# Eight experts worked in an order ranked on the chip, four of them with both halves of their tokens side by side

## The chip, the cores and the metric

The kernel runs on one core of one Trainium2 chip. Its engines are TensorE (PE, with its weight loads as PEld), VectorE (DVE), ScalarE (ACT), GpSimd (POOL) and SyncE (SP), which here only issues transfers. The metric is the time of one execution in device microseconds (us), the median of several runs. The profile is of one execution, whose own time and span are given beside it.

## What is computed

Two layers over 256 latent and 256 context tokens of width 1024. Nearly all of the change lies in the last part of the second layer, a mixture of eight experts of which each token takes two:

```python
def moe_swiglu(h, router, w_gate_up, w_down):
    logits = (h @ router).astype(jnp.float32)
    top_logit, top_idx = lax.top_k(logits, TOP_K)
    top_w = jax.nn.softmax(top_logit, axis=-1)
    gates = jnp.sum(jax.nn.one_hot(top_idx, N_EXPERTS, dtype=jnp.float32) * top_w[..., None], axis=-2).astype(h.dtype)
    out = jnp.zeros_like(h)
    for e in range(N_EXPERTS):
        out = out + gates[..., e:e + 1] * swiglu(h, w_gate_up[e], w_down[e])
    return out
```

`h` is 256 x 1024, an expert's `w_gate_up` 1024 x 7168 and its `w_down` 3584 x 1024, all float32. An expert's weights are 42 tiles of 1 MiB.

## The kernel before

A float32 product is made of three passes: each operand is split into a rounded high half (`fp32r`) and the low rest, and `mm3` (L121) adds hi x hi, hi x lo and lo x hi in PSUM. Weights come through `weights` (L111): a 1 MiB transfer from SyncE into a `raw` tile, a ScalarE copy into `whi` (L108), a VectorE subtraction into `wlo` (L109). In the expert stage there are six raw tiles (one of them in the unused half of `x`) and three pairs of `whi` and `wlo`. SyncE issues in program order and waits for VectorE to have read a raw tile before it fills it again.

In `experts` the router's logits give each token's two experts (`sel`), a count of earlier tokens (`slot`) gives its place in the expert, and `onehot` (L1089) makes from it a 0/1 matrix. `gather` (L1096) multiplies it with the normalized tokens, so that up to 128 of an expert's tokens stand in the columns of `xe` (a high and a low part); `hotT` is its transpose. `run` (L1190) goes through experts 0 to 7 in that order, seven chunks of 512 inner columns each. A chunk is `up` (L1127: gate and up products, 4 x 4 blocks, 48 matmuls of 512 columns), Silu times up into one of two scratch tiles (`spare`, L1083), `turned` (L1147: four transposes and a split into `eahi`, `ealo`) and, one chunk later, `down` (L1156: 24 matmuls into the two banks `y`). In an expert's fifth chunk the next one is gathered; after its last, `finished` and `scatter` add its result, weighted by `gate`, to the tokens in `acc`.

`weigh` (L1052) makes the gate weights and the largest count `mosti`; its small VectorE operations are put among the splits after the first chunk. At the end SyncE and the others read `mosti`, and if an expert has over 128 tokens, the whole round runs a second time (`over` = 1). The order of the instructions on each engine is fixed at build time by a scheduler that follows the program's order and the readiness that it assumes; `issue_after` holds a piece back until a named instruction.

Of the kernel before, what the change touches and what calls it, by code (L numbers as in the profile page):

```python
# [36 lines left out]
EC = DE // 512  # L37
BIG = 3.0e38
# [11 lines left out]
class Trunk:  # L50
# [887 lines left out]
    def experts(self):  # L938
        nc, tc, ins = self.nc, self.tc, self.ins
        with ExitStack() as es:  # L940
# [52 lines left out]
            early = [self.weights(ins["moegu"][0, 0, 0, kh], 2048, pieces=range(4), by=by) for kh, by in ((0, None), (1, nc.gpsimd))]  # L993
# [53 lines left out]
            slot = ew.tile([P, 2, 2, NE], F32, name="slot")  # L1047
            nc.vector.tensor_scalar(slot[:, 1], sel[:, 2], -1000.0, 1000.0, op0=ALU.mult, op1=ALU.add)
            nc.vector.tensor_tensor(slot[:, 0], slot[:, 1], pp[:, :2 * NE].rearrange("p (i e) -> p i e", i=2), op=ALU.add)
            nc.vector.tensor_scalar(slot[:, 1], slot[:, 0], -float(P), None, op0=ALU.add)  # L1050

            def weigh():  # L1052

                for r in range(2):
                    nc.vector.tensor_scalar(sel[:, r], rank, float(r), None, op0=ALU.is_equal)
                top = ew.tile([P, 4, 2], F32, name="top")
                pick = ew.tile([P, 2, NE], F32, name="pick")
# [3 lines left out]
                mx = ew.tile([P, 2], F32, name="mx")  # L1061
                nc.vector.tensor_tensor(mx, top[:, 0], top[:, 1], op=ALU.max)
                for r in range(2):
                    nc.vector.tensor_tensor(top[:, r], top[:, r], mx, op=ALU.subtract)
# [6 lines left out]
                nc.vector.tensor_tensor(gate, sel[:, 0], sel[:, 1], op=ALU.add)  # L1071

                n = self.bank("c")
                nc.tensor.matmul(n[:, :2 * NE], self.ones, both, start=True, stop=True)
                most = ew.tile([P, 48], F32, name="most")[:, :2 * NE + 1]
                nc.vector.tensor_copy(most[:, :2 * NE], n[:, :2 * NE])
                nc.vector.tensor_tensor(most[:, :NE], most[:, :NE], most[:, NE:2 * NE], op=ALU.add)
                nc.vector.reduce_max(most[:, 2 * NE:], most[:, :NE], axis=AX.X)
                nc.vector.tensor_copy(mosti, most[:, 2 * NE:])
# [6 lines left out]

            self.resident.close()
            ex = self.pool(es, "ex")

            def onehot(e, over):  # L1090

                for i in range(2):
                    made = nc.vector.tensor_scalar(hot[:, i], iota, slot[:, over, i, e:e + 1], None, op0=ALU.is_equal)
                return hot, made.ins

            def gather(hot, e):  # L1096

                xe = [t[:, :, e % 2 * P:e % 2 * P + P] for t in self.h]
                for c in range(4):
                    g = self.bank("a")[:, :2 * P].rearrange("p (k n) -> p k n", k=2)  # L1100
                    at = slice(2 * c, 2 * c + 2)
                    for k in range(2):
                        for n, (src, i) in enumerate(((th, 0), (th, 1), (tl, 0), (tl, 1))):
                            nc.tensor.matmul(g[:, k], src[:, i, 2 * c + k], hot[:, i], start=(n == 0), stop=(n == 3))  # L1104
                    if c % 2 == 0:
                        room = spare().rearrange("p (c k n) -> p c k n", c=2, k=2)
                    u = room[:, c % 2]
                    for k in range(2):
                        nc.scalar.activation(u[:, k], g[:, k], AF.Identity, scale=self.mcol(1, 4, 2 * c + k, 0), bias=self.mcol(1, 3, 2 * c + k, 0))
                    nc.scalar.activation(xe[0][:, at], u, AF.Copy)  # L1110
                    self.gathered = nc.vector.tensor_tensor(xe[1][:, at], u, xe[0][:, at].bitcast(F32), op=ALU.subtract).ins
# [7 lines left out]
            def first():  # L1119

                hot, routed = onehot(0, 0)
                with tc.issue_after(routed):
                    for i in range(2):
                        high(1, i)
                        low(1, i)
                return gather(hot, 0), early

            def up(e, c, xe, early=()):
                gu = [self.bank("a") for _ in range(2)]
                for j in range(2):  # L1130
                    for kh in range(2):
                        at = range(4) if (e, c, j) == (NE - 1, EC - 1, 1) else (0,)
# [6 lines left out]
                        for k in range(4):  # L1139
                            kk = kh * 4 + k  # L1140
                            self.mm3(gu[j], [t[:, kk] for t in xe], [t[:, k, :] for t in w], kk == 0, kk == KB - 1)
                sg = spare()
                nc.scalar.activation(sg, gu[0], AF.Silu)
                self.mark = nc.vector.tensor_tensor(sg, gu[1], sg, op=ALU.mult).ins
                return sg

            def turned(sg):  # L1147
                t = self.bank("c")
                for k in range(4):
                    nc.tensor.transpose(t[:, k * P:(k + 1) * P], sg[:, k * P:(k + 1) * P], self.ident)  # L1150
                hi = ex.tile([P, NT], F32R, name="eahi", tag="eahi", bufs=4)
                lo = ex.tile([P, NT], F32R, name="ealo", tag="ealo", bufs=4)
                self.split_into(hi, lo, t)
                return hi, lo
# [71 lines left out]
            with tc.If(n > P):  # L1226
                run(1, gather(onehot(0, 1)[0], 0))
# [101 lines left out]
```

## Time and profile before

| | |
|---|---|
| median of 3 runs | 1993.02 us (1992.82 to 1995.35) |
| profiled execution, own time | 1994.85 us |
| its span | 1993.1 us |
| mean granted clock | 0.985 of full speed |
| TensorE, VectorE, ScalarE busy | 98%, 77%, 56% of the span |
| from HBM | 477.10 MB |

Busy time is the union of an engine's instructions. Matmuls overlap in the record, so one matmul's duration is more than what it adds to the time. The first half of the span holds the other layers, the second half, from about 976 us, the experts. A share of the DMA is the mean busy share of the core's 16 DMA engines.

### The profile page before, as it was taken

To read this page: it belongs to the slowest core of one execution; us is meant where nothing else is said; L and a number is where in the kernel's file an instruction comes from. 1 tells how busy PE (TensorE), PEld (TensorE's weight loads), DVE (VectorE), ACT (ScalarE), POOL (GpSimd) and SP (SyncE) were. 2 spreads that over 40 slices of the span, in tenths; PEclk is the share of its full clock that TensorE was granted. 3 is DMA by queue.
4 is the path that set the end of the run, shared out by engine and by line. 5 is a ranking of instruction groups with operands and counts; after the bars stand their busy time and mean duration, and the time that the engine had idled before them with its cause. 6 is when DMAs were issued, how large, how long until landed. Compare 5 with 4: busy or idle time off the path is not lost.

```text
span 1993.1 us, 29559 instructions
## 1 busy us (share of the span) xinstructions
PE 1950.9 (98%) x11916; PEld 1607.2 (81%) x11916; DVE 1544.0 (77%) x2037; ACT 1113.1 (56%) x1277; POOL 174.3 (9%) x166
## 2 busy tenths in 40 slices
PE   7999999999999999899999999999999999999998
PEld 5888878898888889676888888888888888888886
DVE  4786778586684647676498988989889898898987
ACT  3433332442222124565677777777777777777775
POOL 2233233000000000432300000000000000000000
PEclk8999999999999999998999999999999999999999
DMA  7322223465353432242399999999999999999892
GB/s 270 138 75 85 104 101 128 170 240 203 127 211 130 166 127 75 85 179 102 132 367 346 345 371 341 352 354 346 363 345 360 344 339 371 343 351 353 345 354 97
DMA packets 73809, 480.14 MB, mean 241 GB/s; under 512 B 8768, under 2 KB 11456, under 8 KB 18752
## 3 DMA queue, kind: packets, MB, share of 16 engines
q1 hardware_dynamic: 73664, 478.18, 64.2%
q8 instruction: 95, 1.56, 0.3%
q14 instruction: 50, 0.41, 0.1%
HBM read 477.10 MB, written 1.05 MB: 240 GB/s over the span
## 4 chain that ended last, share of the span: by engine, by line
PE 48%; DVE 2%; DMA 0%; ACT 0%; issue 0%; POOL 0%; DVEq 0%
PE ps_a L124 10%; PE ps_a L125 10%; PE ps_a L123 10%; PE ps_b L124 5%; PE ps_b L125 5%; PE ps_b L123 5%; DVE wlo L109 2%; PE ps_a L1104 1%; PE ps_c L1150 1%; PE ps_a L1185 0%; PE ps_a L1184 0%; ACT whi L108 0%; DVE x L1172 0%; DMA raw<-moegu 0%; DMA raw<-moed 0%
## 5 line engine op out<-in xcount | busy, mean ns | idle before, releaser
L108 ACT ACTIVATE whi<-raw 128x2048 fp32r<-128x2048 f32 (+2 forms) x421 | 708.1, 1694 | 385.8 <-PE ps_a L124 197.9
L109 DVE TENSOR_TENSOR wlo<-raw,whi 128x2048 fp32r<-128x2048 f32 (+2 forms) x389 | 819.8, 2123 | 105.5 <-ACT whi L108 94.2
L123 PE MATMUL ps_a<-whi,hhi 128*128 128x512 f32 (+1 forms) x1168 | 432.0, 370 | 2.0 <-ACT hhi L355 2.0
L125 PE MATMUL ps_a<-whi,hlo 128*128 128x512 f32 (+1 forms) x1168 | 429.9, 369 | 2.4 <-DVE hlo L357 2.4
L124 PE MATMUL ps_a<-wlo,hhi 128*128 128x512 f32 (+1 forms) x1168 | 430.9, 369 | 0.5
L125 PE MATMUL ps_a<-hhi,wlo 128*128 128x512 f32 (+1 forms) x800 | 283.8, 355 | 2.1 <-POOL wlo L109 2.1
L123 PE MATMUL ps_a<-hhi,whi 128*128 128x512 f32 (+1 forms) x800 | 283.4, 357 | 0.8 <-ACT hhi L108 0.7
L124 PE MATMUL ps_a<-hlo,whi 128*128 128x512 f32 (+1 forms) x800 | 283.3, 355 | 0.0
L123 PEld LDWEIGHTS ps_a<-whi,hhi 128*128 128x128 f32 x1168 | 220.7, 189 | 44.3 <-issue 2.9
L125 PEld LDWEIGHTS ps_a<-whi,hlo 128*128 128x128 f32 x1168 | 220.4, 189 | 41.1 <-DVE hlo L357 2.9
L124 PEld LDWEIGHTS ps_a<-wlo,hhi 128*128 128x128 f32 x1168 | 220.8, 189 | 40.6 <-DVE wlo L109 2.4
L124 PE MATMUL ps_b<-wlo,eahi 128*128 128x512 f32 x448 | 177.0, 395 | 0.0
L125 PE MATMUL ps_b<-whi,ealo 128*128 128x512 f32 x448 | 176.9, 395 | 0.0
L123 PE MATMUL ps_b<-whi,eahi 128*128 128x512 f32 x448 | 174.0, 404 | 0.0
L125 PEld LDWEIGHTS ps_a<-hhi,wlo 128*128 128x128 f32 x800 | 152.3, 190 | 23.2 <-POOL wlo L109 2.9
L123 PEld LDWEIGHTS ps_a<-hhi,whi 128*128 128x128 f32 x800 | 151.6, 190 | 22.7 <-ACT hhi L108 1.1
L124 PEld LDWEIGHTS ps_a<-hlo,whi 128*128 128x128 f32 x800 | 152.5, 191 | 19.5
L215 DVE SCALAR_TENSOR_TENSOR junk<-raw,crow 128x1024 f32<-128x1024 f32 x80 | 97.8, 1222 | 31.9 <-DMA raw<-wmod1t 30.7
L125 PEld LDWEIGHTS ps_b<-whi,ealo 128*128 128x128 f32 x448 | 84.2, 188 | 19.7
L124 PEld LDWEIGHTS ps_b<-wlo,eahi 128*128 128x128 f32 x448 | 84.3, 188 | 19.0
L123 PEld LDWEIGHTS ps_b<-whi,eahi 128*128 128x128 f32 x448 | 82.3, 188 | 16.5
L109 DVE TENSOR_TENSOR wlo<-x,whi 128x2048 fp32r<-128x2048 f32 x30 | 68.7, 2289 | 7.8 <-ACT whi L108 6.3
(342 smaller groups left out, 2372.2 us busy)
## 6 DMA issues: line engine op xcount, KB each, us to landing
raw<-moegu SPq DMA_DIRECT2D x202, 1024.0 KB, 6.9
raw<-moed SPq DMA_DIRECT2D x98, 1024.0 KB, 6.8
raw<-wmod SPq DMA_DIRECT2D x26, 1024.0 KB, 6.2
raw<-ffgu SPq DMA_DIRECT2D x22, 1024.0 KB, 4.8
raw<-wmod1t SPq DMA_DIRECT2D x20, 1024.0 KB, 4.8
x<-moegu SPq DMA_DIRECT2D x20, 1024.0 KB, 7.0
raw<-whead SPq DMA_DIRECT2D x14, 768.0 KB, 4.3
x<-moed SPq DMA_DIRECT2D x10, 1024.0 KB, 6.8
```

What stands on the lines that cost most here:

```text
L108: self.nc.scalar.activation(hi[:, at], x[:, at], AF.Copy)
L109: (by or self.nc.vector).tensor_tensor(lo[:, at], x[:, at], hi[:, at].bitcast(F32), op=ALU.subtract)
L123: mm(out, l[0], r[0], start=first, stop=False)
L124: mm(out, l[0], r[1], start=False, stop=False)
L125: mm(out, l[1], r[0], start=False, stop=last)
L215: nc.vector.scalar_tensor_tensor(self.junk, w[:, b], 1.0, self.crow[:, who], op0=ALU.mult, op1=ALU.mult, accum_out=self.mod[1][:, 2 * c + ...
L1104: nc.tensor.matmul(g[:, k], src[:, i, 2 * c + k], hot[:, i], start=(n == 0), stop=(n == 3))
L1150: nc.tensor.transpose(t[:, k * P:(k + 1) * P], sg[:, k * P:(k + 1) * P], self.ident)
```

## The change

The experts are worked in an order that the chip works out. Place 0 is always expert 4 (`FIRST`), whose first weights are loaded before the router is done. The seven others are ranked by token count (`key`, `rk`), and place k takes the rank `RANKS[k]`: the four least loaded come to places 1, 3, 5 and 7, the three others to 2, 4 and 6. `slot`, `gate` and the counts are brought into that order (`ordered`), and seven expert numbers go into registers of SyncE, which adds them to the addresses of the weight transfers (`source`).

At an odd place the expert is light: it holds at most 64 tokens. Its gathered tokens stand once as high parts in 64 columns and once as low parts in the next 64, one stationary block of 128 columns. `add` then makes two passes, with `whi` and with `wlo`; rows 0 to 63 of the result hold the high part's products, rows 64 to 127 the low part's. ScalarE copies both results out, and a product with `fold` (two stacked unit matrices of 64) adds the halves and transposes at once, eight small matmuls where four transposes stood. Silu, product and split then work on 64 columns to a block. If an odd place has over 64 tokens or another over 128, the second round runs.

```diff
+FIRST = 4
+RANKS = (0, 1, 5, 2, 6, 3, 7, 4)
+LIGHT = 64
...
             def weigh():
+                n = self.bank("c")
+                nc.tensor.matmul(n[:, :2 * NE], self.ones, both, start=True, stop=True)
+                few, wide = spare(), spare()
...
+                nc.vector.tensor_tensor(sq, key.unsqueeze(1).to_broadcast([P, NE, NE]), key.unsqueeze(2).to_broadcast([P, NE, NE]), op=ALU.is_lt)
+                nc.vector.tensor_reduce(rk, sq, axis=AX.X, op=ALU.add)
+                for k in range(NE):
+                    nc.vector.tensor_scalar(at[:, k], rk, float(RANKS[k]), None, op0=ALU.is_equal)
+
+                def ordered(out, src):
+                    nc.vector.tensor_tensor(sq, at, src.unsqueeze(1).to_broadcast([P, NE, NE]), op=ALU.mult)
+                    nc.vector.tensor_reduce(out, sq, axis=AX.X, op=ALU.add)
+
+                ordered(key, iota[:, :NE])
+                nc.vector.tensor_copy(ids, key)
...
+                number[1:] = nc.values_load_multi_w_load_instructions(ids[0:1, 1:NE], engines=[mybir.EngineType.SP], min_val=0, max_val=NE - 1)[1]
+
+            def source(name, k, *at):
+
+                if k == 0:
+                    return ins[name][(FIRST,) + at]
+                return ins[name][(bass.ds(number[k], 1),) + at][0]
...
+                if light:
+                    xe = self.h[0][:, :, at]
+                    g = self.bank("a").rearrange("p (d n) -> p d n", d=KB)
+                    u = spare().rearrange("p (d n) -> p d n", d=KB)
+                    for d in range(KB):
+                        for n, (l, r) in enumerate(terms):
+                            nc.tensor.matmul(g[:, d], l[:, d], r[:, :LIGHT], start=(n == 0), stop=(n == 3))
...
+                    nc.scalar.activation(xe[:, :, :LIGHT], u, AF.Copy)
+                    nc.vector.tensor_tensor(xe[:, :, LIGHT:], u, xe[:, :, :LIGHT].bitcast(F32), op=ALU.subtract)
...
+            def add(out, l, r, first, last):
+
+                if isinstance(l, list):
+                    self.mm3(out, l, r, first, last)
+                else:
+                    nc.tensor.matmul(out, l, r[0], start=first, stop=False)
+                    nc.tensor.matmul(out, l, r[1], start=False, stop=last)
...
-                                w = self.weights(ins["moegu"][e, c, j, kh], 2048, pieces=at, loads=at)
+                                w = self.weights(source("moegu", k, c, j, kh), 2048, pieces=at, loads=at)
...
+                both = [spare(), spare()]
+                for j in range(2):
+                    nc.scalar.copy(both[j], gu[j])
+                return both
...
+                    for x, out in zip(sg, (g, u)):
+                        for f in range(4):
+                            nc.tensor.matmul(out[:, f], x[:, f * P:(f + 1) * P], fold, start=True, stop=True)
+                    a = sg[0][:, :256].rearrange("p (f n) -> p f n", f=4)
+                    nc.scalar.activation(a, g, AF.Silu)
+                    nc.vector.tensor_tensor(a, u, a, op=ALU.mult)
+                    self.split_into(hi[:, :, :LIGHT], hi[:, :, LIGHT:], a)
+                    return hi
```

Three places in the order of the instructions. On TensorE at the end of a chunk's `up` in the second expert, before (`ps_a` are the banks of `up`, `ps_b` those of `down`, `hhi` and `hlo` the tokens, `eahi` and `ealo` the chunk ahead):

```order
L123 MATMUL ps_a<-whi,hhi 128x512
L124 MATMUL ps_a<-wlo,hhi 128x512
L125 MATMUL ps_a<-whi,hlo 128x512
L123 MATMUL ps_b<-whi,eahi 128x512
L124 MATMUL ps_b<-wlo,eahi 128x512
L125 MATMUL ps_b<-whi,ealo 128x512
```

and after, the expert at place 1 being light:

```order
L1189 MATMUL ps_a<-whi,hhi 128x512
L1190 MATMUL ps_a<-wlo,hhi 128x512
L1227 MATMUL ps_c<-fold,x 128x64 x4
L1190 MATMUL ps_b<-wlo,eahi 128x512
L1189 MATMUL ps_b<-whi,eahi 128x512
L1190 MATMUL ps_b<-wlo,eahi 128x512 x2
```

The third pass is gone from both products, and the fold products stand among the passes of `down`.

On VectorE behind the first expert's first chunk, where `weigh` runs, before (`x` as an output is the Silu product of L1144 in its scratch tile):

```order
L1064 TENSOR_TENSOR top<-top,mx 128x2 x2
L1144 TENSOR_TENSOR x<-ps_a,x 128x512
L109 TENSOR_TENSOR wlo<-x,whi 128x2048
L1066 TENSOR_TENSOR top<-top 128x2
L109 TENSOR_TENSOR ealo<-ps_c,eahi 128x512
L1067 RECIPROCAL top<-top 128x2
```

and after, the last operations of `weigh` and what stands behind them (`x` as an output of 64 or fewer columns is scratch of the ranking):

```order
L1101 CAST mosti<-x 128x1
L1089 TENSOR_REDUCE gate<-x 128x8
L1088 TENSOR_TENSOR x<-x 128x64
L1089 TENSOR_REDUCE gate<-x 128x8
L113 TENSOR_TENSOR wlo<-raw,whi 128x2048
L1211 TENSOR_TENSOR x<-ps_a,x 128x512 x2
```

The second chunk's product (L1211) no longer stands among the operations of `weigh` but behind the last of them, together with the third chunk's.

On SyncE in the first expert, before:

```order
L100 DMA raw<-moegu 128x2048 x4
L100 DMA raw<-moed 128x2048
L100 DMA x<-moed 128x2048
L100 DMA raw<-moegu 128x2048 x4
L100 DMA raw<-moed 128x2048 x2
```

and after:

```order
L104 DMA raw<-moegu 128x2048 x4
L104 DMA raw<-moed 128x2048
L1119 TENSOR_LOAD ids
L1119 ISA x14
L104 DMA x<-moed 128x2048
L104 DMA raw<-moegu 128x2048 x4
```

The load of the expert numbers, with 14 register instructions, has come ahead of every later weight transfer; from place 1 on one more register instruction (`ISA`) stands ahead of nearly each.

## Rows read from the trace of the kernel before

**Rows 1.** The page, part 1: busy us, share of the span, instructions.

```profile
PE 1950.9 (98%) x11916; PEld 1607.2 (81%) x11916; DVE 1544.0 (77%) x2037; ACT 1113.1 (56%) x1277; POOL 174.3 (9%) x166
```

**Rows 2.** The chain that ended last, second expert on: start us, us, what.

```profile
1331.63 0.44 PE ps_c L1150 x4
...
1348.74 0.44 PE ps_c L1150 x4
...
1439.90 2.85 PE ps_a L1104 x26
...
1565.44 2.85 PE ps_a L1104 x26
```

**Rows 3.** Groups by line, 1010 to 1950 us: count | busy us, mean ns | idle before.

```profile
L108 ACT ACTIVATE whi<-raw 128x2048 fp32r<-128x2048 f32 x289 | 553.9, 1918 | 144.9 <-PE ps_a L125 86.5 <-PE ps_b L125 47.4 <-DMA raw<-moed 7.0
...
L124 PE MATMUL ps_a<-wlo,hhi 128*128 128x512 f32 x845 | 332.3, 393 | 0.5
...
L1143 ACT ACTIVATE x<-ps_a 128x512 f32<-128x512 f32 x53 | 31.8, 601 | 39.8 <-PE ps_a L125 39.8
...
L1186 DVE SCALAR_TENSOR_TENSOR acc<-ps_a,gate,acc 128x512 f32<-128x512 f32 x28 | 19.7, 745 | 0.0
...
L1111 DVE TENSOR_TENSOR hlo<-x,hhi 128x256 fp32r<-128x256 f32 x28 | 10.9, 421 | 2.8 <-ACT hhi L1110 2.8
...
L109 DVE TENSOR_TENSOR ealo<-x,eahi 128x512 fp32r<-128x512 f32 x14 | 9.3, 687 | 0.0
```

**Rows 4.** Waits, 1010 to 1950 us: who waited for whom, total us, times, longest.

```profile
ACT whi L108 <- PE ps_a L125: 94.4, 133, 1.2
...
SPq L100 <- DVE wlo L109: 755.8, 298, 6.1
```

**Rows 5.** Transfers, 1010 to 1950 us: count, size, median us from issue to landing.

```profile
raw<-moegu SPq DMA_DIRECT2D x187, 1024.0 KB, 7.0
```

**Rows 6.** Windows: busy us of each engine, granted clock, DMA share, GB/s.

```profile
20.00:30.00 10.00, 4.49 (x37) 3.30 (x36) 9.96 (x10) 1.35 (x3) 9.02 (x7) 0.78 1.02 402
...
1240.00:1260.00 20.00, 20.00 (x92) 16.32 (x91) 19.22 (x16) 14.03 (x11) 0.00 (x0) 1.00 0.94 359
...
1280.00:1300.00 20.00, 20.00 (x90) 16.29 (x89) 17.39 (x11) 14.54 (x10) 0.00 (x0) 1.00 0.99 383
...
1010.00:1950.00 940.00, 939.53 (x4296) 769.05 (x4295) 824.53 (x525) 697.85 (x529) 0.00 (x0) 1.00 0.94 352
```

**Rows 7.** VectorE in order of time: start us, us, what.

```profile
1010.79 0.15 DVE L1066 TENSOR_TENSOR top<-top 128x2 f32<-128x2 f32 x1
...
1325.79 4.53 DVE L109 TENSOR_TENSOR wlo<-raw,whi 128x2048 fp32r<-128x2048 f32 x2 [0.92 <-ACT whi L108]
```

**Rows 8.** SyncE's queue in order of time, first expert.

```profile
1010.90 0.33 SPq L100 DMA_DIRECT2D x<-moed  x1
1014.51 9.07 SPq L100 DMA_DIRECT2D raw<-moegu  x4
```

**Rows 9.** TensorE in order of time, ahead of the experts and at their start.

```profile
961.04 0.61 PE L978 MATMUL ps_c<-rs,x 128*128 128x8 f32 x4
961.50 0.52 PE L982 MATMUL ps_b<-ident,x 128*128 128x128 f32 x3
...
982.57 0.63 PE L124 MATMUL ps_a<-wlo,hhi 128*128 128x512 f32 x1
983.00 0.63 PE L125 MATMUL ps_a<-whi,hlo 128*128 128x512 f32 x1
...
985.21 0.40 PE L125 MATMUL ps_a<-whi,hlo 128*128 128x512 f32 x1
985.44 0.40 PE L123 MATMUL ps_a<-whi,hhi 128*128 128x512 f32 x1
```

**Rows 10.** Windows of 5 us in the layer before, columns as in rows 6.

```profile
845.00:850.00 5.00, 3.55 (x10) 2.00 (x10) 4.87 (x14) 2.58 (x8) 1.38 (x1) 0.50 0.00 2
...
955.00:960.00 5.00, 4.30 (x35) 4.01 (x35) 1.78 (x4) 1.01 (x2) 1.24 (x1) 1.00 0.51 177
```

More of the change, by code (lines that the diff above doesn't have):

```diff
@@ new lines, in experts, with spare @@
+            nc.vector.tensor_scalar(slot, sel[:, 2], -1000.0, 1000.0, op0=ALU.mult, op1=ALU.add)
+            nc.vector.tensor_tensor(slot, slot, pp[:, :2 * NE].rearrange("p (i e) -> p i e", i=2), op=ALU.add)
+            place = ew.tile([P, 2, 2, NE], F32, name="place")
+            ids = ew.tile([P, NE], I32, name="ids")
+            number = [FIRST] + [None] * (NE - 1)
+            turns = iter(range(1000))
+            def spare():
+                at = D + next(turns) % 2 * NT
+                return rest[:, at:at + NT]
@@ L1078, in weigh @@
-                nc.vector.reduce_max(most[:, 2 * NE:], most[:, :NE], axis=AX.X)
-                nc.vector.tensor_copy(mosti, most[:, 2 * NE:])
-            turns = iter(range(1000))
-            def spare():
-                at = D + next(turns) % 2 * NT
-                return rest[:, at:at + NT]
+                nc.vector.tensor_tensor(byexpert, sel[:, 0], sel[:, 1], op=ALU.add)
+                for i in range(2):
+                    ordered(gate[:, i], byexpert[:, i])
+                number[1:] = nc.values_load_multi_w_load_instructions(ids[0:1, 1:NE], engines=[mybir.EngineType.SP], min_val=0, max_val=NE - 1)[1]
@@ L1096, in gather @@
[L1096 to L1111, printed above, removed]
+                    if light:
+                        made = nc.vector.tensor_scalar(hot[:, i].rearrange("p (a n) -> p a n", a=2), iota[:, :LIGHT].unsqueeze(1).to_broadcast([P, 2, LIGHT]),
+                                                       place[:, 0, i, k:k + 1], None, op0=ALU.is_equal)
+                    else:
+                        made = nc.vector.tensor_scalar(hot[:, i], iota, place[:, over, i, k:k + 1] if k or over else slot[:, i, FIRST:FIRST + 1], None, op0=ALU.is_equal)
@@ L1117, in gather, with up @@
                 return xe, hotT
[L1119 to L1128, printed above, removed]
+            def add(out, l, r, first, last):
+                if isinstance(l, list):
+                    self.mm3(out, l, r, first, last)
+                else:
+                    nc.tensor.matmul(out, l, r[0], start=first, stop=False)
+                    nc.tensor.matmul(out, l, r[1], start=False, stop=last)
+            block = lambda x, f: [t[:, f] for t in x] if isinstance(x, (list, tuple)) else x[:, f]
+            def up(k, c, xe, early=()):
                 gu = [self.bank("a") for _ in range(2)]
@@ L1142, in up @@
[L1142 to L1145, printed above, removed]
+                        for q in range(4):
+                            kk = kh * 4 + q
+                            add(gu[j], block(xe, kk), [t[:, q, :] for t in w], kk == 0, kk == KB - 1)
+                if isinstance(xe, list):
+                    sg = spare()
+                    nc.scalar.activation(sg, gu[0], AF.Silu)
+                    self.mark = nc.vector.tensor_tensor(sg, gu[1], sg, op=ALU.mult).ins
+                    return sg
@@ L1157, in down @@
+                for f in range(4):
+                    nc.tensor.transpose(t[:, f * P:(f + 1) * P], sg[:, f * P:(f + 1) * P], self.ident)
+                lo = ex.tile([P, 4, P], F32R, name="ealo", tag="ealo", bufs=4)
+                self.split_into(*(t.rearrange("p f n -> p (f n)") for t in (hi, lo)), t)
+                return [hi, lo]
+            def down(k, c, act, y, qs):
                 for q in qs:
-                    at = (0, 2, 1, 3) if e == NE - 1 and c >= EC - 2 else (0,)
-                    w = [t.rearrange("p (k n) -> p k n", k=2) for t in self.weights(ins["moed"][e, c, q], 2048, pieces=at, loads=at)]
+                    at = (0, 2, 1, 3) if k == NE - 1 and c >= EC - 2 else (0,)
+                    w = [t.rearrange("p (k n) -> p k n", k=2) for t in self.weights(source("moed", k, c, q), 2048, pieces=at, loads=at)]
@@ L1219, in run @@
                         if c == EC - 3 and e < NE - 1:
[L1220 removed]
+                            ready = gather(e + 1, over)
                 scatter(*due)
[L1223 to L1225 removed]
+            fold = ew.tile([P, LIGHT], F32, name="fold")
+            nc.vector.tensor_tensor(fold, self.ident[:, :LIGHT], self.ident[:, LIGHT:], op=ALU.add)
+            gate, mosti = ew.tile([P, 2, NE], F32, name="gate"), ew.tile([P, 32], I32, name="mosti")[:, :1]
+            run(0, gather(0, 0), early)
+            n = nc.values_load(mosti[0:1, 0:1], min_val=0, max_val=3 * P)
             with tc.If(n > P):
[L1227 removed]
+                run(1, gather(0, 1))
     def run(self):
```

97 lines of the change are left out of this document (59 added, 38 removed).

## The prediction

> **What bounds the kernel now.** I read the page's busy shares first, then the chain, then the expert stage (from about 1000 us to the end) by lines, waits and windows. TensorE is busy 98% of the span [rows 1] and the chain runs through it: seen from the chain, one expert takes 125.54 us (from 1439.90 to 1565.44) and one chunk without a gather 17.11 us (1331.63 to 1348.74) [rows 2]. A chunk has 72 matmuls of 512 columns and four transposes of 0.44 us together, so a matmul costs (17.11 - 0.44) / 72 = 0.2315 us; the 0.393 us that the line shows [rows 3] is overlapped time. The waits agree: ScalarE waits for TensorE to free a split buffer (94.4 us behind `up` alone), and SyncE's queue for VectorE to free a raw tile (755.8 us) [rows 4]. Everything behind TensorE is ready and waits.
>
> But it does not wait long. In the same stage the DMA engines are busy 94% of the time, at 352 GB/s [rows 6], and VectorE 824.5 of 940 us, 88%. That is the point of the case: the change takes work from TensorE alone, and two others stand close behind it.
>
> **What it does, part by part.**
>
> *Tokens.* The reference's inputs send 76, 28, 85, 31, 94, 44, 107 and 47 tokens to the experts in the new order (4, 3, 1, 0, 6, 5, 2, 7), worked out from the reference itself. The odd places hold 64 at most and the even ones 128, so four experts take the light path and the second round is not entered.
>
> *TensorE in a light expert.* Removed: 24 of 72 matmuls a chunk, 168 an expert, 168 x 0.2315 = 38.9 us. Added: eight f32 fold products a chunk instead of four transposes. The nearest row is the router's f32 product with an x block as the stationary side: four records in 0.46 us, two records to a call, 0.23 us a call [rows 9]; with 64 columns rather than 8 I take 0.25, so 56 x 0.25 = 14 us against 28 x 0.11 = 3 us. So TensorE's own time falls from 125.5 to 125.5 - 38.9 + 14 - 3 = 98 us. Were TensorE alone, four experts would give 4 x 27.5 = 110 us.
>
> *VectorE in a light expert.* Its 42 splits stay. Two back to back take 4.53 us, 2.27 each [rows 7]: 95.3 us. The product and the low half are now 256 wide, 14 x 0.42 (the 256-wide row of the gather) = 5.9 us; scatter 4 x 0.745 = 3.0; the four 512-wide operations on the result 4 x 0.687 = 2.7; the next, heavy gather 4 x 0.42 and its `hot`, 2.2 [rows 3]. Sum 109.1 us.
>
> *ScalarE.* 42 x 1.918 = 80.6 us, two copies of 0.60 us a chunk where one Silu stood = 8.4, 14 of 0.42 = 5.9 [rows 3], gather and the rest about 7: 102 us.
>
> *DMA.* An expert is 42 tiles of 1 MiB, 44.04 MB. The stage's mean of 352 GB/s at a share of 0.94 makes 374 at full share, hence 117.6 us; the stretch from 1280 to 1300 us moved 383 at 0.99, hence 115.0; the one from 20 to 30 us, before the experts, 402 at full share, hence 109.6 [rows 6].
>
> So a light expert can't be shorter than VectorE's 109.1 us, and by the DMA rows not longer than 117.6. VectorE's best stretch is 19.22 of 20 us [rows 6]; at that share it needs 109.1 / 0.961 = 113.5 us. Between that and the 115.0 of the DMA I take **114 us**. Raw tiles give a little slack: a slot turns once in six tiles, 6 x 125.54 / 42 = 17.9 us, and a transfer lands 7.0 us after its issue [rows 5], so some two landed tiles lie ready when a light expert begins, and the next heavy one, which asks 2.99 us a tile of a stream that can do 2.74, fills them again. That is why a light expert may run at the DMA's better rows and a heavy one need not pay for it. Gain: 4 x (125.5 - 114) = **46 us**, with bounds of 4 x 7.9 = 32 and 4 x 16.4 = 66.
>
> The Trainium skill's page DMA: Bandwidth & Descriptors, section Specifications, puts a core's share of the memory at about 358 GB/s. By that a light expert would take 123.0 us, and the change would be worth some 10 us. The 383 and 402 GB/s of [rows 6] are against it, but those are stretches of 10 and 20 us, and a rival below is built on it.
>
> *Ranking on VectorE.* Behind the first chunk of the first expert stood 20 small operations, now 50. One takes about 0.16 us [rows 7], so 30 x 0.16 = 4.8 us more. They use both of the two scratch tiles (`spare`) that the next chunks' products need, so in the order the second product now stands behind the last of them and the second chunk's transposes behind the third chunk's matmuls. VectorE has some 12% of slack there, TensorE none to give back. I take 4 us; bounds 0 (the slack takes it) and 9 (nothing hides it, and ScalarE's Silu holds the splits behind it).
>
> *Expert numbers on SyncE.* The load of the seven numbers and 14 register instructions stand ahead of the transfer that was issued at 1010.90 us, the next at 1014.51 [rows 8]. SyncE now waits for VectorE to make the numbers, by the order a few small operations behind the one that stood at 1010.79 us [rows 7], some fifteen of the new ones ahead of it, so about 1013 to 1015 us. Behind it queue all later weight loads. The two transfers come up to 4 us late, and the two landed tiles (6 us) cover that: 0, at most 4. Each of the 294 transfers of places 1 to 7 has one register instruction ahead. No row here prices it; transfers are due every 2.74 us at the fastest and SyncE's issue takes 0.33 [rows 8], so anything under 2 us is hidden. 0.
>
> *Heavy experts.* Same matmuls in the same line. They gather for a light one, 32 matmuls of 64 columns for 32 of 128 (26 records 2.85 us, so 3.5 for 32 [rows 2], at most halved): -0.5 each, between -1.7 and 0. A light expert may hand over with fewer tiles ready: +1 each, between 0 and 2. Together +2. The end (last matmul to last store) keeps its form: 0.
>
> **Sum**, on the profiled execution: span 1993.1, less 46, plus 4, plus 2 = 1953. The span stands 0.1 us from the median of the three timed runs (1993.02), so no correction.
>
> **The rivals.**
>
> *The stream has no more to give.* If the 352 GB/s of the stage is already what the memory yields over 100 us, a light expert takes 44.04 / 0.352 = 125.1 us and TensorE's gain turns into a wait for raw tiles. Time 1993 - 2 + 6 = 1997; half way to my forecast 1975. For it: a share of 0.94 with SyncE always waiting to issue. Against it: the 383 and 402. (The skill's figure above lies in this case, at 1989.) 0.16.
>
> *TensorE's gain in full.* VectorE and the DMA overlap better than their best rows, and light experts near 100 us: 1993 - 102 + 6 = 1897. It needs 440 GB/s, above every row. Light experts at 106 us would give 1921. 0.06.
>
> *The clock falls: slower.* TensorE, now waiting some 14% of a light expert in short pieces, could drop to 1.2 GHz. At 982.57 us, right after a thin stretch, matmuls stand 0.43 us apart instead of 0.2315 [rows 9]. The windows show both: 3.55 us busy of 5 at a granted clock of 0.50, 4.30 of 5 at 1.00 [rows 10]; a light expert has 4.3 of 5. At half clock its 336 matmuls alone take 144 us, with the rest about 170. It turns into a loss once (125.5 - 98) / 72 = 38% of the work runs slow; at half of it, 134 us, the time is 1993 + 34 + 6 = 2033. Against it: a slow TensorE is a full one, and at 985.21 us the spacing was back at 0.23 [rows 9], some 7 us after the slow matmuls began. The Trainium skill's TensorE: Matmul & The Clock Gate, section Loop structure matters more than you think, names waits for transfers between matmuls as what drops the clock. It speaks against this change; by it the sum would be the 2033 just worked out. 0.06.
>
> *It doesn't do what it says.* Were a light place given over 64 tokens, the whole second round would run, some 990 us more. The counts exclude it unless the chip ranks otherwise. 0.02.
>
> **How the numbers follow.** Forecast 0.70 (1932 to 1972), no more from the stream 0.16 (1972 to 1999), full gain 0.06 (1890 to 1932), half clock 0.06 (2000 to 2060), second round 0.02. The range of 8 in 10 is the forecast's own and 10 us of the case of the stream: 1932 to 1982. A measurement can tell about 0.2%, 4 us. Faster by more: 0.70 + 0.06 + 0.11 of the stream = 0.87; within: 0.04; slower: 0.09 (half clock, second round, 0.01 of the stream).
>
> **What would show it.** Right: experts at odd places 110 to 118 us, even ones 125 to 127; DMA share 0.97 or more in both; TensorE waiting on `wlo` or `whi` in light experts at a granted clock of 1.00; VectorE over 92% there; VectorE's chain after the first chunk some 5 us longer. Wrong: a light expert at 98 to 105 us (the DMA rows were no ceiling and VectorE's sum too large), or above 120 with the DMA at full share and under 365 GB/s (the stream), or with VectorE and the DMA both below 90% (the fixed order of three split buffers, which I have priced only through VectorE's best stretch); heavy experts above 128 us (tiles not made up); a stall of more than 9 us between 1000 and 1030 us.

## The result, and the profile after

The changed kernel takes 2013.5 us (2011.1 to 2015.5) where the kernel before, timed beside it, takes 1994.2 (1992.8 to 1996.1): a ratio of 1.0096, 95% interval 1.0078 to 1.0113. It is slower; the forecast of 1953 us was wrong in its sign.

From the page before, the head of part 4 (shares of the chain that ended last) and VectorE's splits in part 5 (out<-in, count | busy us, mean ns | idle before, and what ended it):

```profile
PE 48%; DVE 2%; DMA 0%; ACT 0%; issue 0%; POOL 0%; DVEq 0%
...
L109 DVE TENSOR_TENSOR wlo<-raw,whi 128x2048 fp32r<-128x2048 f32 (+2 forms) x389 | 819.8, 2123 | 105.5 <-ACT whi L108 94.2
```

and from the page after, with part 1 to lay beside [rows 1] and a group of TensorE's:

```profile
PE 1874.9 (93%) x11580; PEld 1513.5 (75%) x11580; DVE 1522.9 (76%) x2053; ACT 1114.8 (55%) x1321; POOL 174.3 (9%) x166
...
PE 26%; DVE 13%; ACT 5%; DMA 5%; issue 4%; POOL 0%; DVEq 0%; ACTq 0%
...
L113 DVE TENSOR_TENSOR wlo<-raw,whi 128x2048 fp32r<-128x2048 f32 (+2 forms) x389 | 817.5, 2121 | 143.0 <-ACT whi L112 136.7
...
L1190 PE MATMUL ps_a<-wlo,hhi 128*128 128x512 f32 x448 | 186.9, 417 | 46.5 <-DVE wlo L113 46.4
```

TensorE's busy time fell by 76 us and the time rose: so it now waits, and the chain, which ran almost through TensorE alone, passes through VectorE, ScalarE and the DMA too. Before its 448 matmuls with `wlo` for `up` in the light experts TensorE sat idle for 46.4 us in all; VectorE, which makes `wlo`, waited 136.7 us for `whi`, 94.2 before the change; ScalarE makes `whi`. To see in which experts, the result's addition to `acc` marks each expert on VectorE. Its first record for places 4, 5 and 6 (start us, us, what):

```profile
1634.52 0.74 DVE L1268 SCALAR_TENSOR_TENSOR acc<-ps_a,gate,acc 128x512 f32<-128x512 f32 x1
...
1772.96 2.72 DVE L1268 SCALAR_TENSOR_TENSOR acc<-ps_a,gate,acc 128x512 f32<-128x512 f32 x4
...
1893.87 0.75 DVE L1268 SCALAR_TENSOR_TENSOR acc<-ps_a,gate,acc 128x512 f32<-128x512 f32 x1
```

The stretch before the light one's mark is 138.4 us long, the next 120.9, and they repeat (138.45 and 120.9 from 1375.17 us). Because the marks move a little against the experts, I compare the pair: 259.35 us, where the kernel before needs 1879.49 - 1628.40 = 251.1 for the same two marks. Only the first light stretch is short, 124.6 us. The windows of those stretches (columns as in [rows 6]):

```profile
1254.00:1375.00 121.00, 116.89 (x541) 94.19 (x539) 103.33 (x65) 87.82 (x69) 0.00 (x0) 1.00 0.93 347
1375.00:1513.00 138.00, 115.19 (x523) 87.57 (x524) 110.82 (x73) 97.96 (x85) 0.00 (x0) 0.99 0.87 335
...
1634.00:1772.00 138.00, 115.12 (x524) 87.26 (x523) 111.17 (x73) 98.29 (x86) 0.00 (x0) 0.99 0.91 333
```

VectorE's work in a light stretch, 110.8 us, is what the prediction added up (109.1), ScalarE's 98 too (102), and no engine is full over the stretch: VectorE 80%, the DMA 87 to 91% at 333 to 335 GB/s. In two whole chunks of it, 1650.90 to 1687.84 us, the DMA share is 0.95 and 0.96 at 336 and 341 GB/s, so the share alone doesn't clear the transfers; run 11 does. The granted clock is 0.99. It fell for a moment, in the chunk in which the next expert is gathered:

```profile
1705.00:1710.00 5.00, 2.38 (x8) 1.42 (x8) 3.62 (x7) 5.00 (x8) 0.00 (x0) 1.00 0.89 357
1712.00:1715.40 3.40, 3.40 (x12) 2.81 (x11) 3.40 (x3) 2.05 (x2) 0.00 (x0) 0.50 0.97 393
```

After a piece in which TensorE was busy 2.38 of 5 us the clock stands at 0.50, the lower level of 1.2 GHz, for 3.4 us. By my estimate, half of those 3.4 us, that costs TensorE some 1.7 us; the prediction's rival for a loss, a clock that falls for much of a light expert, did not come. In the stretch from 1634 us ScalarE's order of time shows why nobody is full (idle before, and who ended it, in brackets; `COPY` is L1215, the copy of the gate product or the `up` product out of PSUM):

```profile
1644.53 3.71 ACT L112 ACTIVATE whi<-raw 128x2048 fp32r<-128x2048 f32 x2
1650.90 0.58 ACT L1215 COPY x<-ps_a 128x512 f32<-128x512 f32 x1 [2.67 <-PE ps_a L1190]
1651.39 3.72 ACT L112 ACTIVATE whi<-raw 128x2048 fp32r<-128x2048 f32 x2
1657.61 0.59 ACT L1215 COPY x<-ps_a 128x512 f32<-128x512 f32 x1 [2.50 <-PE ps_a L1190]
1658.09 1.92 ACT L112 ACTIVATE whi<-raw 128x2048 fp32r<-128x2048 f32 x1
```

and VectorE beside it:

```profile
1646.63 4.49 DVE L113 TENSOR_TENSOR wlo<-raw,whi 128x2048 fp32r<-128x2048 f32 x2
1653.34 4.49 DVE L113 TENSOR_TENSOR wlo<-raw,whi 128x2048 fp32r<-128x2048 f32 x2 [2.22 <-ACT whi L112]
1660.04 2.29 DVE L113 TENSOR_TENSOR wlo<-raw,whi 128x2048 fp32r<-128x2048 f32 x1 [2.21 <-ACT whi L112]
```

The copy stands at the head of ScalarE's queue and waits for TensorE's last matmul of the product. That matmul waits for VectorE's `wlo`. VectorE has one split's work left, 2.2 us, and then waits for the split that stands behind the copy. There are two such rounds a chunk. The 2.2 us follow from the ring: from the end of a `wlo` (half way through the first record, about 1648.88) it takes 2.0 us for its 8 matmuls until the copy begins (1650.90), 0.5 for the copy and 1.9 for the next split until VectorE can go on (1653.34), 4.5 us in all, of which it fills 2.2. A chunk has 13.2 us of splits, 0.8 of small work and twice 2.2 idle, 18.4 us; between the same issues of SyncE's queue I read 18.5. The waits from 1640 to 1772 us say the same in sums (total us, times, longest):

```profile
ACT x L1215 <- PE ps_a L1190: 24.7, 10, 2.9
DVE wlo L113 <- ACT whi L112: 22.2, 13, 2.2
PEld ps_a L1190 <- DVE wlo L113: 15.3, 13, 2.1
```

The fold products wait for the copies too, in TensorE's queue, but they are not what holds the ring:

```profile
1651.54 1.10 PE L1227 MATMUL ps_c<-fold,x 128*128 128x64 f32 x8 [0.44 <-ACT x L1215]
1652.46 0.47 PE L1190 MATMUL ps_a<-wlo,hhi 128*128 128x512 f32 x1
...
1655.68 0.50 PE L1190 MATMUL ps_a<-wlo,hhi 128*128 128x512 f32 x1 [1.13 <-DVE wlo L113]
```

Behind them TensorE works off the next tile and then waits again for VectorE's `wlo`.

The first light expert shows the same code without the wait, and the step from one to the other. ScalarE, then VectorE:

```profile
1156.85 0.57 ACT L1215 COPY x<-ps_a 128x512 f32<-128x512 f32 x1
...
1161.68 0.57 ACT L1215 COPY x<-ps_a 128x512 f32<-128x512 f32 x1
...
1169.23 0.58 ACT L1215 COPY x<-ps_a 128x512 f32<-128x512 f32 x1 [0.32 <-PE ps_a L1190]
...
1174.58 0.58 ACT L1215 COPY x<-ps_a 128x512 f32<-128x512 f32 x1 [2.95 <-PE ps_a L1190]
```

```profile
1153.52 11.09 DVE L113 TENSOR_TENSOR wlo<-raw,whi 128x2048 fp32r<-128x2048 f32 x5
...
1177.01 2.29 DVE L113 TENSOR_TENSOR wlo<-raw,whi 128x2048 fp32r<-128x2048 f32 x1 [2.85 <-ACT whi L112]
```

In the first four light chunks five splits follow each other without a gap, and a chunk takes 13.9 us (from one chunk's product of Silu and `up` to the next, 1150.62 to 1164.53); then the copies begin to wait. The order on ScalarE differs there: counted by the buffers' numbers in the program, three splits (once five) lie between a product's last split and its copy in those four chunks, and one (in places two) in all later ones. I call this number the **lead** of the copy. It is the scheduler's choice; the source doesn't ask for it.

### The profile page after: what moved, and what is told of

It is laid out like the page before. It is cut to its first block, busy times and chain, and to the rows that moved or that the text cites. A ratio compares the mean times of both kernels' runs of the same rounds, so it can differ in the third digit from the quotient of the medians.

```text
span 2009.3 us, 29618 instructions
## 1 busy us (share of the span) xinstructions
PE 1874.9 (93%) x11580; PEld 1513.5 (75%) x11580; DVE 1522.9 (76%) x2053; ACT 1114.8 (55%) x1321; POOL 174.3 (9%) x166
## 4 chain that ended last, share of the span: by engine, by line
PE 26%; DVE 13%; ACT 5%; DMA 5%; issue 4%; POOL 0%; DVEq 0%; ACTq 0%
DVE wlo L113 10%; PE ps_a L128 5%; PE ps_a L129 5%; PE ps_a L127 5%; ACT whi L112 4%; DMA raw<-moed 2%; DMA raw<-moegu 2%; PE ps_a L1190 2%; PE ps_b L129 2%; PE ps_b L128 2%; PE ps_b L127 2%; PE ps_a L1189 1%; DVE acc L1268 1%; PE ps_a L1158 1%; PE ps_c L1234 0%
## 5 line engine op out<-in xcount | busy, mean ns | idle before, releaser
L113 DVE TENSOR_TENSOR wlo<-raw,whi 128x2048 fp32r<-128x2048 f32 (+2 forms) x389 | 817.5, 2121 | 143.0 <-ACT whi L112 136.7
L128 PE MATMUL ps_a<-wlo,hhi 128*128 128x512 f32 (+1 forms) x720 | 256.0, 356 | 9.2 <-DVE wlo L113 9.2
L127 PE MATMUL ps_a<-whi,hhi 128*128 128x512 f32 (+1 forms) x720 | 256.3, 356 | 2.3 <-ACT hhi L359 2.0
L129 PE MATMUL ps_a<-whi,hlo 128*128 128x512 f32 (+1 forms) x720 | 253.9, 353 | 2.4 <-DVE hlo L361 2.4
L1190 PE MATMUL ps_a<-wlo,hhi 128*128 128x512 f32 x448 | 186.9, 417 | 46.5 <-DVE wlo L113 46.4
L1189 PE MATMUL ps_a<-whi,hhi 128*128 128x512 f32 x448 | 178.4, 400 | 3.9 <-ACT whi L112 3.9
L128 PEld LDWEIGHTS ps_a<-wlo,hhi 128*128 128x128 f32 x720 | 136.7, 190 | 31.7 <-DVE wlo L113 14.3
L127 PEld LDWEIGHTS ps_a<-whi,hhi 128*128 128x128 f32 x720 | 136.7, 190 | 25.4 <-issue 2.9
L129 PEld LDWEIGHTS ps_a<-whi,hlo 128*128 128x128 f32 x720 | 136.3, 190 | 19.8 <-DVE hlo L361 2.9
L129 PE MATMUL ps_b<-whi,ealo 128*128 128x512 f32 x224 | 87.5, 392 | 0.2 <-DVE ealo L113 0.2
```

The costliest lines, as they stand in the source:

```text
L113: (by or self.nc.vector).tensor_tensor(lo[:, at], x[:, at], hi[:, at].bitcast(F32), op=ALU.subtract)
L127: mm(out, l[0], r[0], start=first, stop=False)
L128: mm(out, l[0], r[1], start=False, stop=False)
L129: mm(out, l[1], r[0], start=False, stop=last)
L1189: nc.tensor.matmul(out, l, r[0], start=first, stop=False)
L1190: nc.tensor.matmul(out, l, r[1], start=False, stop=last)
```

## The experiments

All are compared with runs of the kernel before on the same chip, 1994.3 to 1995.3 us.

**1. Both copies later.** The gate product's copy is held behind `up`'s fourth split, the `up` product's copy and the fold behind `down`'s second:

```
+                        if (j, kh) == (1, 1) and not isinstance(xe, list):
+                            g = spare()
+                            with tc.issue_after(self.split):
+                                nc.scalar.copy(g, gu[0])
...
+                    with tc.issue_after(self.split):
+                        nc.scalar.copy(sg[1], up1)
```

> Theory A (head of ScalarE's queue): in a light expert each chunk has two copies out of PSUM that wait for TensorE's last matmul of a product while the next split stands behind them; VectorE then has no high half to work on and stands still for 2.2 us, twice a chunk, 18.46 us a chunk in the changed kernel. This kernel changes nothing but where the copies stand: the gate product's copy behind the fourth split of `up`, the up product's copy and the fold behind the second split of `down`, one tile later each. A expects VectorE's 2.2 us gaps gone, a light chunk at 14 (VectorE alone) to 16.4 us (the stream at 383 GB/s), two neighbouring experts together in 235 to 246 us instead of 259.3, and 1935 to 1970 us in all. Theory B (the memory stream gives no more than some 350 GB/s): a chunk of 6.29 MB stays at 17.9 us or more and the time at 2000 or more. Theory C (three split buffers): the split that now passes the copy waits for a buffer instead, the chunk gains under 1 us, over 2000 us.

Measured: 1951.1 us (1949.0 to 1953.3), ratio 0.9783 (0.9767 to 0.9799). Moving two copies of 0.6 us in the order is worth 62 us. The pair takes 241.9.

**2. Only the gate product's copy later**, the first half of that edit.

> Only the gate product's copy goes one split later; the up product's copy and the fold stay as in the changed kernel. A expects one of the two 2.2 us gaps of a chunk to go: a light chunk near 16.3 us, two experts together near 245 us, 1965 to 1990 us in all, about half of what both copies give. B and C: no gain, 2005 to 2018.

Measured: 1987.7 us (1987.0 to 1990.2), ratio 0.9968 (0.9953 to 0.9982); the pair takes 252.6. One of the two waits a chunk goes, and with it less than half of the gain: the loop still closes once a chunk.

**3. Ranking without light experts.** The experts run in the new order, with numbers from registers, but all on the old path (`light = False`).

> The ranked order, the expert numbers in registers and the ranking on VectorE stay; no expert is light, all eight take three passes. Measures ranking and register addresses by themselves. A expects the kernel before plus 0 to 5 us (1993 to 1999), since at the end of the first expert's scatter the changed kernel is less than 1 us behind. Theory D (register-addressed transfers slow the weight stream): 2004 us or more, and more idle time of SyncE's queue between transfers.

Measured: 1981.3 us (1979.1 to 1985.1), ratio 0.9928 (0.9912 to 0.9945). A surprise: an expert takes 123.9 us instead of 125.5 with the same matmuls. Runs 5 to 8 look for the cause.

**4. Numbers written in the program**, all else as changed:

```
-                return ins[name][(bass.ds(number[k], 1),) + at][0]
+                return ins[name][((4, 3, 1, 0, 6, 5, 2, 7)[k],) + at]
```

> The changed kernel with the expert numbers written into the program in the order in which the chip ranks these inputs, so no load of numbers and no register instruction on SyncE; the ranking on VectorE stays, and the light experts are as in the changed kernel. A: 2005 to 2016 us, as the changed kernel. D: below 2000 us.

Measured: 2005.8 us (2004.4 to 2009.1), ratio 1.0061 (1.0044 to 1.0077): 7.7 us less. They lie mostly in the first light stretch, 117.9 us instead of 124.6; all later pairs are alike (259.6). The order has moved there as well: in the fifth light chunk the copy of the `up` product has a lead of 2, where the changed kernel has 1, and waits 0.62 us for TensorE where 2.95 stood above (1174.58):

```profile
1173.78 0.59 ACT L1212 COPY x<-ps_a 128x512 f32<-128x512 f32 x1 [0.62 <-PE ps_a L1187]
```

So this run changed the numbers and the order at once; run 9 parts them.

**5. The kernel before, one small buffer wider.** Beside the tensors that matter, rank_only shares with the changed kernel that the expert stage's small buffers take 128 bytes more, and the third pair of split buffers, `eahi`, `ealo`, `hotT` and one raw tile lie 128 bytes higher. So I widened one in the kernel before:

```
-                most = ew.tile([P, 48], F32, name="most")[:, :2 * NE + 1]
+                most = ew.tile([P, 80], F32, name="most")[:, :2 * NE + 1]
```

> The kernel before, unchanged but for one small SBUF buffer of the expert stage made 128 bytes wider (most, 48 to 80 columns), so that the third pair of split buffers, the activations of the experts and the turned one-hot matrices stand at the addresses that they have in rank_only. The experts keep their order 0 to 7. If rank_only's shorter experts (123.6 us where the kernel before has 125.4) come from where these buffers lie: experts of 123.3 to 123.9 us, TensorE's matmuls of a chunk 0.2275 us apart, 1993 less 7 times 1.6 = about 1982 (1979 to 1985). If they come from the order of the experts or their data, or from source addresses taken from a register: 1993 to 1996 and 125.4 us an expert.

Measured: 1980.0 us (1979.3 to 1982.9), ratio 0.9928 (0.9914 to 0.9942), the same as rank_only, and experts of 123.9 us. TensorE in order of time, twelve matmuls apart, the kernel before and then this one:

```profile
1639.82 0.39 PE L124 MATMUL ps_a<-wlo,hhi 128*128 128x512 f32 x1
...
1642.61 0.39 PE L124 MATMUL ps_a<-wlo,hhi 128*128 128x512 f32 x1
```

```profile
1639.70 0.39 PE L123 MATMUL ps_a<-whi,hhi 128*128 128x512 f32 x1
...
1642.42 0.39 PE L123 MATMUL ps_a<-whi,hhi 128*128 128x512 f32 x1
```

2.79 us against 2.72: 0.2325 us a matmul against 0.2267. The kernel before has stretches at either pitch, this one nearly everywhere the shorter (short pieces at 0.231 to 0.235 remain, around 1663 us for one). So the changed kernel carries a gain that has nothing to do with its idea.

**6 and 7. Other places.** The same buffer 64 bytes wider; and the small buffers 128 bytes smaller (`most` of 17 columns, `mx` inside `top`).

> The kernel before with the same small buffer 64 bytes wider instead of 128. The third pair of split buffers stood at 0 modulo 256 in the kernel before and stands at 128 in before_pad, as the other two pairs do in all kernels; here it stands at 64. If only an odd multiple of 128 helps: 1993 to 1995 and TensorE's matmuls 0.231 us apart in places. If leaving the multiple of 256 is enough: 1979 to 1983.

> The kernel before with the same small buffers 128 bytes smaller, so that the third pair of split buffers, the activations and the one-hot matrices lie 128 bytes lower, again at 128 modulo 256. If the place modulo 256 decides: 1979 to 1983, as before_pad. If it is the one address of before_pad, or that anything moved up: 1993 to 1996.

Measured: 64 bytes 1994.9 us, ratio 0.9998 (0.9989 to 1.0008), nothing; 128 bytes lower 1980.3 us, ratio 0.9928 (0.9911 to 0.9944), the whole gain. The third pair begins at byte 145152 in the kernel before, 0 modulo 256, and the other two pairs at 128 modulo 256. At 128 modulo 256 the kernel is fast, on either side; at 0 and at 64 it is slow. `eahi`, `ealo`, `hotT` and one raw tile moved along with the pair in every one of these runs, so which of them decides is not shown, and which engines meet there stays open.

**8. The changed kernel, and copy_late, at the old places** (the largest count shares the buffer of the numbers, 128 bytes less):

> The changed kernel with the expert stage's small buffers cut by 128 bytes (the largest count shares the buffer of the numbers), so that the third pair of split buffers, the activations and the one-hot matrices stand where the kernel before has them. Widening them by as much in the kernel before gave 14 us. Placement theory: each of the four heavy experts, at TensorE's bound, pays 1.2 to 1.6 us, the light ones nothing: 2013.5 plus 5 to 6 = 2018 to 2020 (copy_late paid 5.0). Otherwise 2011 to 2015.

> copy_late (1951.1 us) with the same 128 bytes taken out again (the largest count shares the buffer of the expert numbers), so that the third pair of split buffers, the activations and the one-hot matrices stand where the kernel before has them. Placement theory: the heavy experts are at TensorE's bound and pay 1.5 to 2 us each again, the light ones, which are not, nothing or little: 1951 plus 6 to 14 = 1957 to 1965, heavies of 122 to 123 us. Rival (order or data): 1949 to 1953, heavies of 120.7.

Measured: the changed kernel 2020.5 us (2020.2 to 2022.5), 7 more; copy_late 1956.1 (1955.5 to 1957.0), 5 more. Heavy stretches are longer in both (122.06 for 120.9, and 122.06 for 120.7). In copy_late the light ones give as much back, its pair stays at 241.9, and its 5 us are there by the second mark. So the change alone costs about 25 us (2020.5 against 1995.3), and the places hid 7 of them.

**9. copy_late with the numbers in the program.**

> copy_late with the experts' numbers written in the program: no load of numbers on SyncE, no register in a source address; all else as in copy_late. In the changed kernel the same edit gave 7.7 us (2013.5 to 2005.8), seen in the first experts. Theory (SyncE's stop for the numbers in expert 0 delays a chain of transfers once, 4 to 8 us): 1943 to 1948. Rival (those 7.7 us came from how the stalls of the light chunks happen to fall): 1949 to 1953.

Measured: 1952.4 us (1948.5 to 1953.1), against 1951.1. Loading the numbers and addressing by register cost nothing that can be measured. So what run 4 gained goes with the lead of the copies in the first light expert.

**10. Half the bytes.** The light experts' transfers bring the first half of each weight block, and the splits read it twice, so that all engines work as before; the light experts' output is another one. In copy_late and in the changed kernel:

```
+            r = self.raw(src[:, :n // 2], n // 2)
...
+            x = r.unsqueeze(1).to_broadcast([P, 2, n // 2])
```

> copy_late, where the light experts' transfers bring only the first half of each weight block (0.5 MB instead of 1 MB), and the split reads that half twice, so that ScalarE, VectorE and TensorE do as much work as before; the output of the light experts is therefore another one. It asks what bounds copy_late's light chunk (17.2 us; DMA engines 96% busy, VectorE 90%, TensorE 91%). If the stream binds: the light expert falls towards VectorE's 109.4 us of work or lower, so 121.1 to 110-112, three to four of them: 1915 to 1930. If the order on ScalarE and VectorE binds: 1944 to 1951, with VectorE still waiting for whi in every chunk.

> The changed kernel, where the light experts' transfers bring only the first half of each weight block and the split reads that half twice (the output of the light experts is therefore another one); the same edit took copy_late from 1951 to 1916 us. If the light chunk of 18.4 us is set by ScalarE's order (the two copies that wait for TensorE at the head of its queue, with the next splits behind them), it stays: 2000 to 2014 us, VectorE idle about 2.2 us twice a chunk. If the stream sets it: the light experts get 8 to 11 us shorter each, 1970 to 1985.

Measured: 1916.1 us (1915.1 to 1919.1) and 1918.9 us (1917.7 to 1919.3). The second fell by 95 us, against what I expected of it: by this run alone the transfers would have been the cause. But the order on ScalarE had moved as well: in nearly every light chunk of both kernels the scheduler put the copies at a lead of 3 (presumably since it counts with the transfers' size). The edit had changed two things.

**11 and 12. Bytes and order apart.** half_one is after_half with the copies held to a lead of exactly 1 in all 28 light chunks (each copy behind the next split, and the split after that behind the copy). copy_three brings all bytes and holds the copies, and with the second one the fold, to a lead of 3 (2 in places).

> after_half (half of each light expert's bytes, 1919 us) with one thing added: ScalarE's copies are held to exactly one split behind their product's last one in all 28 light chunks; in after_half they came to stand three behind, since the build-time scheduler orders by the transfers it assumes. The output of the light experts is another one, as in after_half. Queue theory: the light chunk is 18.4 us again though half the bytes move, VectorE idle 2.2 us twice a chunk for whi; with the first four light chunks slow as well, 2013 plus 0 to 18: 2010 to 2032. If the transfers decided: 1917 to 1930.

> The changed kernel with its two copies held back further than in copy_late: the number of splits on ScalarE between the last split of a product and that product's copy is 3 in nearly all light chunks (1, in places 2, in the changed kernel; 2 in copy_late; 3 in the first four light chunks of all of them, where a chunk took 13.5 to 14 us). All bytes are loaded. Queue theory: no copy waits for TensorE any more, so the light chunk is left to the stream and VectorE: a light expert of 113 to 117 us at 380 to 400 GB/s, pair of 234 to 238 where copy_late has 241.8, 1930 to 1941. If copy_late's light experts are already at the stream's rate: 1948 to 1953, pair of 241 to 243.

half_one measured 2011.9 us (2010.9 to 2013.7), ratio 1.0086 (1.0070 to 1.0101). Its VectorE, and its window of a light stretch:

```profile
1651.87 4.49 DVE L128 TENSOR_TENSOR wlo<-raw,whi 128x2048 fp32r<-128x2048 f32 x2
1658.55 4.49 DVE L128 TENSOR_TENSOR wlo<-raw,whi 128x2048 fp32r<-128x2048 f32 x2 [2.19 <-ACT whi L127]
1665.23 2.29 DVE L128 TENSOR_TENSOR wlo<-raw,whi 128x2048 fp32r<-128x2048 f32 x1 [2.19 <-ACT whi L127]
```

```profile
1640.00:1772.00 132.00, 112.39 (x506) 83.30 (x505) 108.36 (x73) 95.17 (x85) 0.00 (x0) 1.00 0.69 239
```

The DMA engines are idle a third of the time, the granted clock is 1.00, and still there are the same 2.2 us twice a chunk and the same 18.4 us from one restart of VectorE to the same one of the next chunk (1658.55 to 1677.00). So the order alone makes the stall. That the totals agree as well is partly chance: the first light stretch takes 131.55 us here (124.6 in the changed kernel, whose first four chunks have the longer lead), and the pair, with half the bytes, 254.9 instead of 259.4.

copy_three measured 1948.9 us (1947.6 to 1950.8), ratio 0.9769 (0.9756 to 0.9782), no better than copy_late as far as the intervals tell. Its windows of a heavy and a light stretch, and after_half's of a light one:

```profile
1487.00:1602.00 115.00, 113.47 (x530) 92.36 (x528) 99.50 (x61) 84.54 (x64) 0.00 (x0) 1.00 0.93 352
1607.00:1722.00 115.00, 104.89 (x500) 83.52 (x500) 106.80 (x71) 94.37 (x85) 0.00 (x0) 0.99 0.97 383
```

```profile
1597.00:1697.00 100.00, 95.04 (x462) 76.33 (x461) 96.96 (x63) 87.70 (x78) 0.00 (x0) 1.00 0.80 294
```

With the order mended and all bytes, the stream is full (0.97); with the order mended and half the bytes, VectorE is (97 of 100 us). These are the bounds that the prediction named, and the changed kernel reaches neither. In a table (the pair is the time between the marks of places 4 and 6, a light and a heavy stretch):

| kernel | lead of the two copies in later light chunks | bytes of a light expert | pair, us | time, us |
|---|---|---|---|---|
| before | no copies | all | 251.1 | 1994 |
| changed | 1, in places 2 | all | 259.4 | 2013.5 |
| half_one | 1 | half | 254.9 | 2011.9 |
| copy0_late | 2 and 1 | all | 252.6 | 1987.7 |
| copy_late | 2 | all | 241.9 | 1951.1 |
| copy_three | 3, in places 2 | all | 239.6 | 1948.9 |
| after_half | 3 | half | 230.9 | 1918.9 |
| copy_late_half | 3 | half | 230.4 | 1916.1 |

## Why the prediction was wrong

**The step that failed is the light expert's 114 us.** It was chosen between VectorE's 109.1 and the DMA's 117.6, as if the longest sum of work set the time. The paragraph on ScalarE priced "two copies of 0.60 us a chunk where one Silu stood" at 8.4 us an expert and asked what they take, and not what they wait for and what is queued behind them. The kernel before already held the hint: its one Silu in that place sat idle 39.8 us for TensorE over 53 times [rows 3], 0.75 us each. That was harmless while TensorE was the last to finish, and there was one a chunk. Behind a TensorE with a third less to do it closes a ring: copy, split, `wlo`, matmul, copy, 18.4 us a chunk. Counted by the pair, 259.35 us stand where the prediction has 114 and 126, 240. Twice 19.35, 5.5 in the first pair (245.5 from the first mark to the third) and some 14 in the last stretch (106.1, where the 103.6 of the kernel before less a light expert's 11.5 follows from the forecast) make 58 of the 60.5 us that the forecast missed by. copy_three's pair is 239.6.

**The sums were right.** VectorE's 109.1 was measured as 110.8, ScalarE's 102 as 98, a fold product's 0.25 as 0.23 (four, of two records each, from 1651.54 to 1652.46), and the stream's 115.0 as 115 us at 383 GB/s and a share of 0.97 in copy_three. With the order mended, the kernel takes 1949 to 1951 us, and the forecast was 1953. With the buffers at their old places, as the forecast had them, copy_late takes 1956.1.

**What the prediction listed as a sign against itself came true**: a light expert above 120 us with VectorE and the DMA both below or near 90% ("the fixed order of three split buffers, which I have priced only through VectorE's best stretch"). It stood there without a price or a chance of its own. The order of ScalarE's queue could have been read before the run, since it is fixed in the program; the ring above needs no number that the kernel before didn't show.

**The rivals.** That the stream has no more to give than 352 GB/s is refuted: 383 over 115 us. The Trainium skill's page DMA: Bandwidth & Descriptors, section Specifications, puts a core's share at about 358 GB/s, half of what it gives a stack for two cores; this kernel runs on one core, the measurement is above the share, and it decides. But the stream is what stops copy_three (half the bytes at the same lead gain another 30 us). TensorE's gain in full was out of reach by VectorE's 97%. The granted clock stayed at 0.99 to 1.00 in all light stretches shown, with TensorE busy 83% (changed kernel) to 95% (after_half) of them. It did fall, to 0.50 for 3.4 us, behind the gap shown above, and the stall doesn't need it: half_one's light stretch has 1.00 and the same 18.4 us. The Trainium skill's page TensorE: Matmul & The Clock Gate, section Loop structure matters more than you think, names long waits for transfers between all matmuls as what makes TensorE go cold; the waits in the ring are pieces of about 1 us, for `wlo`, and in those chunks the clock stayed at 1.00 (1650.90 to 1687.84).

**The small terms.** The numbers on SyncE, forecast 0: no difference that the runs can tell where the order is mended (run 9), 7.7 in the changed kernel, where the order moved too (run 4). The ranking, forecast 4: rank_only against before_pad, which has the same places, 1.3 us with overlapping intervals. The heavy experts, forecast +2: their stretches became shorter, 120.9 us; 1.2 of that is the buffers' places (run 8), the rest not separated, since the marks shift against the experts.

## What to carry to other kernels

When a change takes work from the engine that all others wait for, go through the in-order queues of the next engines and ask of each instruction that reads the first engine's result what stands behind it: two copies of 0.6 us, each with a split behind it, cost 4.4 us a chunk, and moving them one split back gained 62 us. A change of one size can move the whole order of a scheduled kernel, so read the order again before laying a difference to that size (run 10). And a new buffer moves those behind it: test a gain of under 1% with the same places on both sides.

## What the runs showed of the hardware

The place of buffers in SBUF changed the pitch of matmuls: with the third pair of split buffers, and the four kinds of buffers that moved along with it, at 128 modulo 256 bytes, like the other two pairs, twelve matmuls of 512 columns took 2.72 us, and at 0 modulo 256 up to 2.79; the whole kernel takes 1980 us instead of 1994 to 1995, with nothing else changed but a small buffer's width (run 5). At 64 modulo 256 nothing was gained. Which of these buffers decides, and why, is not settled by these runs.
